# Expert stage: the split weights' tiles kept beside the load buffers, 14 load buffers in place of 15

## The chip, the cores and the metric

One core of a Trainium2 chip runs the whole program. The metric is the device time of one execution in microseconds (us), as the median of several runs. The engines are named as the profile names them: PE is TensorE's matmul, PEld its weight load, DVE is VectorE, ACT is ScalarE, POOL is GpSimd, SP is SyncE, which here issues the large loads.

## What is computed

The program is a two-block transformer over 256 tokens of width 1024. The first block has two layers (attention with a gated MLP, pooling, and a product-key expert layer each); the second block has a hybrid attention layer and, last of all, a mixture of 32 experts. Only that last stage changes its work, so it is the part of the reference that must be seen:

```python
def hier_moe(v, w_grp, b_grp, w_exp, b_exp, w_gate, w_up, w_down):
    ...
    w = p_grp * p_in / jnp.sum(p_in, axis=-1, keepdims=True)
    expert_id = g_sel * MOE_EXPERTS_PER_GROUP + e_sel
    combine = jnp.einsum('tk,tke->te', w, jax.nn.one_hot(expert_id, MOE_N_EXPERTS, dtype=f32))
    y = jnp.zeros(vt.shape, f32)
    for e in range(MOE_N_EXPERTS):
        hdn = jax.nn.silu(vt @ w_gate[e]) * (vt @ w_up[e])
        y = y + (combine[:, e:e + 1].astype(hdn.dtype) * hdn) @ w_down[e]
    return y.reshape(bsz, seq, d).astype(v.dtype)
```

Each token picks one of 4 groups and 2 of the group's 8 experts. A final root-mean-square norm follows.

## The kernel before, in words

**Weights before the expert stage.** Every large weight matrix comes in pieces of 128 partitions by 2048 columns (1024 KB). `raw` (L157) takes one of 3 load buffers of the pool `raw_p` and issues the load on SP's queue. `halves` (L164) cuts a piece in two and `split` (L148) writes each half as two rounded parts, a high one (ACT, L149) and a low one (DVE, L150), into tiles `hi` and `lo` of the pool `hl_p` (3 of each, 128 by 1024, 24 KB a partition in all). The last piece of work of this kind is `mix_out`, which multiplies by `w_out` (4 pieces) and computes the routing logits.

**Where the tiles lie.** `raw_p` is the second pool from the left end of the memory; `hl_p` stands at the right end (`side="right"`) in a stack of its own, `hl_es`, and is closed just before the expert stage. The stage's pool `rpool` then takes everything to the right of the room that is still in use: 10 load buffers `w0` to `w9`, and the rounded tiles `G`, `GT` and `yr`. `Carve` (L31) is a small allocator that cuts tiles out of large tiles that exist already; the other tiles of the stage are cut that way out of rooms of the layers before.

**The expert stage, `moe` (L1443).** The weights of 32 experts are 6 pieces each, 192 loads of 1024 KB, all on SP's queue, issued by `load` (L1458) in the order in which they are used. Load `j` goes into buffer `j` modulo the length of a ring `buf`: 3 of `raw_p`, 10 of `rpool`, 2 of the room, which are 15. A load waits on SP's queue until PE has done the last matmul on the buffer's old contents, and loads behind it wait with it.

The experts are done in 16 pairs, n = 0 to 15. Two experts of 64 token places each share the 128 columns of TensorE: `e = 0` works on the left half, `e = 1` on the right. One pair is, on PE:

- H, `hidden` (L1587): 32 matmuls for gate and up, 4 units of 2 loads each;
- S, `scatters` (L1621): 8 matmuls that add the pair before to the token sums;
- G, `places` and `gather` (L1551): 32 matmuls that gather the tokens of the next four experts, in every second pair (even n below 14);
- T, `hid_T` (L1598): 4 transposes, which need DVE's product of gate and up (L1592);
- B, `back` (L1569, L1571): 4 small matmuls for the pair after;
- D, `down` (L1611): 16 matmuls, 2 units of 2 loads; ACT (L1614) and DVE (L1615) write the two rounded halves of each result, which S reads.

Each matmul of H and D leaves two records in the trace, so that D is 32 records.

**What sets the order.** The program is written in the order H, S, G, T, B, D, but a scheduler orders the instructions of each engine when the kernel is built, by its own estimates of when operands are ready. It is free to put the S and G of a pair between the matmuls of D and H, and PE then runs its queue strictly in that order. The same scheduler orders SP's queue. After the 16 pairs a conditional block (L1668) handles experts with more than 64 tokens; here it is skipped. `final` (L1699) norms and writes the output.

Of the kernel before, what the change touches and what calls it, by code (L numbers as in the profile page):

```python
# [9 lines left out]
F32 = mybir.dt.float32  # L10
F32R = mybir.dt.float32r
# [6 lines left out]
P = 128  # L18
T = 256
# [11 lines left out]
class Carve:  # L31


    def __init__(self, *ranges):
        self.free, self.tags = [[t, lo * 256, hi * 256] for t, lo, hi in ranges], {}

    def tile(self, shape, dt=F32, name=None, tag=None, bufs=1):
        n = int(np.prod(shape[1:]))
        tag = tag or name
        if tag not in self.tags:  # L40
            w = -(-n // 8) * 8
            fits = [r for r in self.free if r[2] - r[1] >= w * bufs]
            assert fits, (name, n, [r[2] - r[1] for r in self.free])
            r = fits[0]
            self.tags[tag] = [r[0], r[1], w, bufs, 0]
            r[1] += w * bufs
        t = self.tags[tag]
        base, lo, w, bufs, j = t
        assert n <= w, (name, n, w)
        t[4] = (j + 1) % bufs  # L50
        v = base[:shape[0], lo + j * w:lo + j * w + n]
        if dt != F32:
            v = v.bitcast(dt)
        if len(shape) > 2:
            ax = "abcdefg"[:len(shape) - 1]
            v = v.rearrange(f"p ({' '.join(ax)}) -> p {' '.join(ax)}", **dict(zip(ax, shape[1:])))
        return v
# [45 lines left out]
class Net:  # L103
    def __init__(self, es, tc, A):
        self.tc, self.nc, self.A = tc, tc.nc, A
        nc = self.nc
        ep = es.enter_context
        self.cpool = ep(tc.tile_pool(name="cpool", bufs=1))
        self.raw_p = ep(tc.tile_pool(name="raw_p", bufs=3))
        self.hl_es = ExitStack()  # L110
        self.hl_p = self.hl_es.enter_context(tc.tile_pool(name="hl_p", bufs=3, side="right"))
        self.rings()
        self.ps = ep(tc.tile_pool(name="ps", bufs=4, space=bass.MemoryType.PSUM))
        self.small = ep(tc.tile_pool(name="small", bufs=2))
        self.hhl_p = ep(tc.tile_pool(name="hhl_p", bufs=1))
        self.hh, self.hl = (self.hhl_p.tile([P, KD, T], F32R, name=n) for n in ("hh", "hl"))
        self.uid = 0
        c = self.cpool
        self.ident = c.tile([P, P], F32, name="ident")
        self.ones = c.tile([P, P], F32, name="ones")  # L120
        self.vecs = c.tile([P, NV], F32, name="vecs")
        self.mod = [c.tile([P, 48], F32, name=f"mod{l}") for l in range(2)]
        self.mhalf = c.tile([P, 2], F32, name="mhalf")
        nc.scalar.dma_start(self.vecs, A["vecs"])
        nc.scalar.dma_start(self.ident, A["ident"])
        self.iota = c.tile([P, P], F32, name="iota")
        nc.scalar.dma_start(self.iota, A["iota"].partition_broadcast(P))
        nc.vector.memset(self.ones, 1.0)
        nc.vector.memset(self.mhalf, -0.5)

        self.scr = None
# [1311 lines left out]
    def moe(self, x, state, pool, rpool, nring):  # L1443

        nc, A, tc = self.nc, self.A, self.tc
        mm = nc.tensor.matmul
        tl = lambda shape, name, dt=F32, tag=None: pool.tile(shape, dt, name=name, tag=tag or name)
        CAP = 64
# [2 lines left out]
        xf, parts, pl, br, tri = state  # L1451


        buf = [None] * 3 + [rpool.tile([P, 2048], F32, name=f"w{j}") for j in range(nring)]
        buf += [pool.tile([P, 2048], F32, name=f"w{nring + j}") for j in range(2)]
        nring = len(buf)
# [99 lines left out]
        xg_tags = cycle(("vT", "xg"))  # L1556

        def tiles(ne):
            return (rpool.tile([P, 2, ne, CAP], F32R, tag="G", bufs=2, name=self.nm("G")),
                    pool.tile([P, KD, ne, CAP], F32, tag=next(xg_tags), name=self.nm("xg")))  # L1560

        def back(G, cb):

            GT = rpool.tile([P, T], F32R, tag="GT", bufs=2, name=self.nm("GT"))
            cw = pool.tile([P, 1], F32, tag="cw", bufs=2, name=self.nm("cw"))
            ps = self.mm()
            pair = lambda tt: G[:, tt].bitcast(F32).rearrange("p e s -> p (e s)")
            for tt in range(2):
                nc.tensor.transpose(ps[:, tt * P:(tt + 1) * P], pair(tt), self.ident)  # L1569
            for tt in range(2):  # L1570
                mm(ps[:, T:T + 2], pair(tt), cb[:, tt], start=(tt == 0), stop=(tt == 1))  # L1571
            nc.vector.tensor_copy(GT, ps[:, :T])
            for e in range(2):
                o = slice(e * CAP, (e + 1) * CAP)
                nc.vector.tensor_copy(cw[o], ps[o, T + e:T + e + 1])
            return GT, cw

# [25 lines left out]
        def down(hT, W, cw):  # L1603

            ys = []
            for n in range(2):
                ps = self.mm()
                Ws = [next(W) for _ in range(2)]
                for f in range(4):
                    for e in range(2):  # L1610
                        mm(ps[e * CAP:(e + 1) * CAP, :], hT[:, f, e, :], Ws[e][:, f * 512:(f + 1) * 512],  # L1611
                           start=(f == 0), stop=(f == 3))
                y = rpool.tile([P, 2, 512], F32R, tag="yr", bufs=3, name=self.nm("y"))
                nc.scalar.activation(y[:, 0, :], ps, AF.Copy, scale=cw)  # L1614
                nc.vector.scalar_tensor_tensor(y[:, 1, :], ps, cw, y[:, 0, :].bitcast(F32), ALU.mult, ALU.subtract)  # L1615
                ys.append(y)
            return ys

        def scatter(a, GT, y, tt, start, stop):
            for j in range(2):  # L1620
                mm(a, GT[:, tt * P:(tt + 1) * P], y[:, j, :], start=start and j == 0, stop=stop and j == 1)  # L1621

# [19 lines left out]

        def scatters(n, GT, ys):
            for m, y in enumerate(ys):
                for tt in range(2):
                    scatter(accs[tt][m], GT, y, tt, n == 0, n == 15)
                if n == 15:
                    add(accs, m)

        for n in range(16):  # L1650
# [4 lines left out]
            GT, cw = bk  # L1655
# [3 lines left out]
            if n < 15:  # L1659
                m = n + 1  # L1660
                p = slice(2 * (m % 2), 2 * (m % 2) + 2)
# [6 lines left out]
        with tc.If(over > CAP):  # L1668
            with tc.For_i(0, 32, 1) as ei:
# [4 lines left out]
                for b in (1, 3):  # L1674
# [10 lines left out]
                    G, xg = tiles(2)  # L1685
# [4 lines left out]
                    GT, cw = back(G, cb2)  # L1690
# [142 lines left out]
def build(tc, A, out):  # L1833
    nc = tc.nc
    with ExitStack() as es:
        net = Net(es, tc, A)
# [13 lines left out]
        with tc.tile_pool(name="mix0", bufs=1) as pool:  # L1850
            net.scr = pool
            x = pool.tile([P, 2, D], F32, name="x")
# [20 lines left out]
        pool = Carve((net.S2[0], 24, 64), whole[1])  # L1873
# [9 lines left out]
        x, gb = net.ahead  # L1883
# [10 lines left out]
        pool = Carve(*whole)  # L1894
# [6 lines left out]
        x, gb = net.ahead  # L1901
# [17 lines left out]
        for tt in range(2):  # L1919
            a, b = q[:, tt:tt + 1], q[:, 2 + tt:3 + tt]  # L1920
# [11 lines left out]
        pool = Carve((net.S2[0], 8, 64))  # L1932
        state = net.mix_out(x, pool)
        ws.close()
        upper.close()
        net.hl_es.close()
        with tc.tile_pool(name="moe", bufs=1, reuse_waits="tile") as rpool:
            net.moe(x, state, pool, rpool, 10)
            net.final(x, out, pool)


# [13 lines left out]
```

## Time and profile before

| | |
|---|---|
| median of 3 runs | 2654.69 us (2653.91 to 2655.37) |
| the profiled execution's own time | 2655.24 us |
| its span, first to last instruction | 2653.5 us |
| PE busy over the span | 2556.4 us (96%) |
| DVE, ACT busy | 1672.7 us (63%), 1267.6 us (48%) |
| bytes moved | 598.26 MB, mean 225 GB/s |
| expert stage, first matmul of H to last S | about 2160 to 2641 us of the span |

The span is shorter than the execution's own time by 1.7 us, which lie around it. A share of busy time is an average over stages with different limits, so the expert stage is read by itself: by the idle time of PE and what ended it, by SP's queue, and by PE's instructions in order of time.

### The profile page before, as it was taken

Reading aid. Unit: us, or ns where it says so; the run is one execution under the profiler, and the core shown is the slowest. Engines: PE = TensorE matmul, PEld = TensorE weight load, DVE = VectorE, ACT = ScalarE, POOL = GpSimd, SP = SyncE. Lnnn points to the kernel's source line nnn. Section 1 sums busy time; section 2 is a strip of 40 time slices with the busy share of each in tenths; the row PEclk is TensorE's granted clock in tenths of the full one; section 3 lists DMA queues with packets and bytes.
Section 4 is the critical chain, followed back from the end, with each engine's and each line's share of the span. In section 5 each row is a group of like instructions: output and inputs, shape, how many; then the busy total and the mean of one; then the engine's idle time right before and its main releaser. Section 6 shows DMA issues by size and latency. Waiting matters only on the chain. (4 is left out here: it accounts for less than half of the span.)

```text
span 2653.5 us, 39872 instructions
## 1 busy us (share of the span) xinstructions
PE 2556.4 (96%) x15570; PEld 2053.0 (77%) x15570; DVE 1672.7 (63%) x3465; ACT 1267.6 (48%) x2335; POOL 24.6 (1%) x28
## 2 busy tenths in 40 slices
PE   8989999999999998999999999999899989999997
PEld 4679999999888887999999988888777854333332
DVE  3665998889669985499888966666677631111111
ACT  4544445887545544444588754445466521001010
POOL 0000000000000000000000000000000000000000
PEclk9999999999999999999999999999999989999999
DMA  6544555333669972454533365555442589999994
GB/s 256 201 164 169 180 182 184 132 139 128 237 224 391 374 262 82 160 190 175 191 128 136 136 218 196 183 196 197 144 162 97 185 349 421 421 417 402 411 412 185
DMA packets 86798, 598.26 MB, mean 225 GB/s; under 512 B 10431, under 2 KB 12367, under 8 KB 15695
## 3 DMA queue, kind: packets, MB, share of 16 engines
q1 hardware_dynamic: 80608, 583.73, 58.5%
q10 hardware_dynamic: 5998, 11.94, 1.3%
q8 instruction: 124, 2.03, 0.3%
q14 instruction: 68, 0.55, 0.1%
HBM read 592.49 MB, written 3.15 MB: 224 GB/s over the span
## 5 line engine op out<-in xcount | busy, mean ns | idle before, releaser
L150 DVE TENSOR_TENSOR lo<-raw,hi 128x1024 fp32r<-128x1024 f32 x580 | 705.9, 1219 | 286.3 <-ACT hi L149 282.9
L149 ACT CAST hi<-raw 128x1024 fp32r<-128x1024 f32 x580 | 604.0, 1044 | 463.4 <-PE mm L737 289.4
L736 PE MATMUL mm<-hh,hi 128*128 128x256 f32 x2048 | 589.2, 288 | 0.0
L738 PE MATMUL mm<-hh,lo 128*128 128x256 f32 x2048 | 580.4, 283 | 0.0
L737 PE MATMUL mm<-hl,hi 128*128 128x256 f32 x2048 | 580.1, 283 | 0.0
L174 PE MATMUL acc<-hi,hh 128*128 128x512 f32 (+1 forms) x1312 | 511.3, 394 | 2.1 <-ACT hh L149 1.6
L176 PE MATMUL acc<-hi,hl 128*128 128x512 f32 (+1 forms) x1312 | 511.9, 390 | 0.0
L175 PE MATMUL acc<-lo,hh 128*128 128x512 f32 (+1 forms) x1312 | 511.2, 390 | 0.0
L737 PEld LDWEIGHTS mm<-hl,hi 128*128 128x128 f32 x2048 | 393.4, 192 | 0.0
L736 PEld LDWEIGHTS mm<-hh,hi 128*128 128x128 f32 x2048 | 393.1, 192 | 0.0
L738 PEld LDWEIGHTS mm<-hh,lo 128*128 128x128 f32 x2048 | 392.8, 192 | 0.0
L174 PEld LDWEIGHTS acc<-hi,hh 128*128 128x128 f32 x1312 | 247.4, 189 | 53.7 <-issue 2.2
L176 PEld LDWEIGHTS acc<-hi,hl 128*128 128x128 f32 x1312 | 247.2, 188 | 49.6
L175 PEld LDWEIGHTS acc<-lo,hh 128*128 128x128 f32 x1312 | 247.7, 189 | 48.7 <-DVE lo L150 0.6
L149 ACT CAST hh<-room 128x256 fp32r<-128x256 f32 x272 | 109.4, 407 | 311.2 <-PE acc L175 302.6
L1587 PE MATMUL mm<-w,room 128*64 128x512 f32 x688 | 181.9, 595 | 0.0
L1592 DVE TENSOR_TENSOR room<-room,mm 128x512 f32<-128x512 f32 x16 | 11.0, 688 | 267.2 <-PE mm L1587 267.2
L150 DVE TENSOR_TENSOR hl<-room,hh 128x256 fp32r<-128x256 f32 x272 | 112.0, 423 | 88.1 <-ACT hh L149 87.3
L1614 ACT ACTIVATE y<-mm,room 128x512 fp32r<-128x512 f32 x32 | 22.0, 687 | 248.8 <-PE mm L1611 248.8
L788 PE MATMUL mm<-room 128*128 128x128 f32 x1024 | 132.1, 275 | 0.1
L1587 PEld LDWEIGHTS mm<-w,room 128*64 128x64 f32 x688 | 56.1, 137 | 91.9 <-issue 89.4
L788 PEld LDWEIGHTS mm<-room 128*128 128x128 f32 x1024 | 123.9, 192 | 0.5 <-ACT room L782 0.5
(467 smaller groups left out, 3072.3 us busy)
## 6 DMA issues: line engine op xcount, KB each, us to landing
w<-in_moe SPq DMA_DIRECT2D x129, 1024.0 KB, 11.2
raw<-in_dn SPq DMA_DIRECT2D x128, 1024.0 KB, 4.9
raw<-in_up SPq DMA_DIRECT2D x103, 1024.0 KB, 4.9
raw<-in_moe SPq DMA_DIRECT2D x39, 1024.0 KB, 10.4
room<-in_up SPq DMA_DIRECT2D x25, 1024.0 KB, 6.3
raw<-in_modt SPq DMA_DIRECT2D x24, 1024.0 KB, 6.7
room<-in_moe SPq DMA_DIRECT2D x24, 1024.0 KB, 10.7
raw<-in_w2in SPq DMA_DIRECT2D x18, 1024.0 KB, 4.8
```

The source lines that it names most:

```text
L149: self.nc.scalar.copy(hi, src)
L150: self.last_lo = self.nc.vector.tensor_tensor(lo, src, hi.bitcast(F32), ALU.subtract).ins
L174: mm(ps, xh, wh, start=start, stop=False)
L175: mm(ps, xh, wl, start=False, stop=False)
L176: mm(ps, xl, wh, start=False, stop=stop)
L736: mm(o, wh, hh[:, k, :], start=(k == 0), stop=False)
L737: mm(o, wh, hl[:, k, :], start=False, stop=False)
L738: mm(o, wl, hh[:, k, :], start=False, stop=(k == KD - 1))
L788: mm(ps[:, j * P:(j + 1) * P], B[:, j, :], Am[:, j, :], start=True, stop=True)
L1587: mm(ps[e * CAP:(e + 1) * CAP, :], xs[:, k, e, :], Ws[e][:, (k % 4) * 512:(k % 4 + 1) * 512], start=(k == 0), stop=(k == KD - 1))
L1592: nc.vector.tensor_tensor(g, g, out[1], ALU.mult)
L1614: nc.scalar.activation(y[:, 0, :], ps, AF.Copy, scale=cw)
```

## The change

1. `hl_p` is opened on the left, right behind `raw_p`, for the whole program; `hl_es` and its closing are gone. All pools that are opened later lie 24 KB further right.
2. In the expert stage the 3 `hi` and 3 `lo` tiles of `hl_p` are taken once and stay. `y` takes the `hi` tiles in turn; `G` and `GT` are cut out of the `lo` tiles by `Carve`, 2 of each, as many as before.
3. `rpool` holds load buffers alone, 9 in place of 10, so the ring is 3 + 9 + 2 = 14, and the loads run 12 ahead in place of 13 as the program is written.
4. `Carve.tile` compares the type with that of the tile that it cuts from, since `lo` is not of type f32.

```diff
--- before.py
+++ after.py
@@ -49,7 +49,7 @@
         assert n <= w, (name, n, w)
         t[4] = (j + 1) % bufs
         v = base[:shape[0], lo + j * w:lo + j * w + n]
-        if dt != F32:
+        if dt != base.dtype:
             v = v.bitcast(dt)
         if len(shape) > 2:
             ax = "abcdefg"[:len(shape) - 1]
@@ -107,8 +107,7 @@
         ep = es.enter_context
         self.cpool = ep(tc.tile_pool(name="cpool", bufs=1))
         self.raw_p = ep(tc.tile_pool(name="raw_p", bufs=3))
-        self.hl_es = ExitStack()
-        self.hl_p = self.hl_es.enter_context(tc.tile_pool(name="hl_p", bufs=3, side="right"))
+        self.hl_p = ep(tc.tile_pool(name="hl_p", bufs=3))
         self.rings()
         self.ps = ep(tc.tile_pool(name="ps", bufs=4, space=bass.MemoryType.PSUM))
         self.small = ep(tc.tile_pool(name="small", bufs=2))
@@ -1451,6 +1450,11 @@
         xf, parts, pl, br, tri = state
 
 
+        his, los = ([self.hl_p.tile([P, 1024], F32R, tag=t, name=self.nm(t)) for _ in range(3)] for t in ("hi", "lo"))
+        rt = Carve(*[(t, 0, 4) for t in los])
+        ybuf = cycle(his)
+
+
         buf = [None] * 3 + [rpool.tile([P, 2048], F32, name=f"w{j}") for j in range(nring)]
         buf += [pool.tile([P, 2048], F32, name=f"w{nring + j}") for j in range(2)]
         nring = len(buf)
@@ -1556,12 +1560,12 @@
         xg_tags = cycle(("vT", "xg"))
 
         def tiles(ne):
-            return (rpool.tile([P, 2, ne, CAP], F32R, tag="G", bufs=2, name=self.nm("G")),
+            return (rt.tile([P, 2, ne, CAP], F32R, tag="G", bufs=2, name=self.nm("G")),
                     pool.tile([P, KD, ne, CAP], F32, tag=next(xg_tags), name=self.nm("xg")))
 
         def back(G, cb):
 
-            GT = rpool.tile([P, T], F32R, tag="GT", bufs=2, name=self.nm("GT"))
+            GT = rt.tile([P, T], F32R, tag="GT", bufs=2, name=self.nm("GT"))
             cw = pool.tile([P, 1], F32, tag="cw", bufs=2, name=self.nm("cw"))
             ps = self.mm()
             pair = lambda tt: G[:, tt].bitcast(F32).rearrange("p e s -> p (e s)")
@@ -1610,7 +1614,7 @@
                     for e in range(2):
                         mm(ps[e * CAP:(e + 1) * CAP, :], hT[:, f, e, :], Ws[e][:, f * 512:(f + 1) * 512],
                            start=(f == 0), stop=(f == 3))
-                y = rpool.tile([P, 2, 512], F32R, tag="yr", bufs=3, name=self.nm("y"))
+                y = next(ybuf).rearrange("p (a d) -> p a d", a=2)
                 nc.scalar.activation(y[:, 0, :], ps, AF.Copy, scale=cw)
                 nc.vector.scalar_tensor_tensor(y[:, 1, :], ps, cw, y[:, 0, :].bitcast(F32), ALU.mult, ALU.subtract)
                 ys.append(y)
@@ -1933,9 +1937,8 @@
         state = net.mix_out(x, pool)
         ws.close()
         upper.close()
-        net.hl_es.close()
         with tc.tile_pool(name="moe", bufs=1, reuse_waits="tile") as rpool:
-            net.moe(x, state, pool, rpool, 10)
+            net.moe(x, state, pool, rpool, 9)
             net.final(x, out, pool)
```

No instruction of computation is added or removed. Lines of the changed kernel are 4 higher in `moe` (L1587 is L1591 there).

**SP's queue where the stage's loads begin.** Behind the last piece of `w_out` stand, before (`raw` are the 3 shared load buffers, `w_20285` to `w_20294` the buffers w0 to w9):

```order
L1462 DMA raw_20408<-in_moe 128x2048
L1462 DMA raw_20410<-in_moe 128x2048
L1462 DMA raw_20412<-in_moe 128x2048
L1462 DMA w_20285<-in_moe 128x2048
L1462 DMA w_20286<-in_moe 128x2048
L1462 DMA w_20287<-in_moe 128x2048
```

and with the change (`w_20290` to `w_20298` are w0 to w8):

```order
L1466 DMA w_20290<-in_moe 128x2048
L1466 DMA w_20291<-in_moe 128x2048
L1466 DMA raw_20410<-in_moe 128x2048
L1466 DMA w_20292<-in_moe 128x2048
L1466 DMA raw_20412<-in_moe 128x2048
L1466 DMA raw_20414<-in_moe 128x2048
L1466 DMA w_20293<-in_moe 128x2048
```

Three loads into `rpool` now stand ahead of the last `raw` loads, whose buffers the last pieces of `w_out` still fill. After w8 SP now also reads the count that the conditional block tests (L1671); before, it did so after the last load.

**PE's queue in pair 2, from the middle of H to D.** Before, S (`acc`) and G (`G_20706`) lie inside H:

```order
L1587 MATMUL mm_20654<-w_20293,room_1438 64x512
L1621 MATMUL acc_20351<-y_20637,GT_20519 128x512 x2
...
L1621 MATMUL acc_20354<-y_20651,GT_20519 128x512 x2
L1587 MATMUL mm_20654<-w_20294,room_1438 64x512
...
L1587 MATMUL mm_20675<-room_1438 64x512
L1551 MATMUL mm_20709<-G_20706,hh 128x256 x2
...
L1587 MATMUL mm_20675<-room_1438 64x512 x7
L1551 MATMUL mm_20729<-G_20706,hh 128x256 x2
...
L1587 MATMUL mm_20675<-raw_20589,room_1438 64x512
L1598 MATMUL mm_20749<-ident,room_1438 128x128 x4
```

With the change H runs through, then S, then all of G, then T:

```order
L1591 MATMUL mm_20669<-w_20290,room_1438 64x512
L1625 MATMUL acc_20355<-hi_20286,lo_20288 128x512 x2
...
L1625 MATMUL acc_20358<-hi_20284,lo_20288 128x512 x2
L1555 MATMUL mm_20704<-lo_20287,hh 128x256 x2
...
L1555 MATMUL mm_20734<-lo_20287,hl 128x256 x2
L1602 MATMUL mm_20744<-ident,room_1438 128x128 x4
L1573 MATMUL mm_20750<-ident,lo_20287 128x128 x2
```

The stretch of a pair is counted here from the first matmul of the D before it to that of its own D. In counts of matmuls, the stretch of pair 2 was D16 H9 S8 H8 G20 H7 G4 H1 G8 H7 T4 and is D16 H32 S8 G32 T4.

**PE's queue in pair 3, around the end of D.** Before, S is cut in two, one half inside D and one behind the first matmul of H:

```order
L1611 MATMUL mm_20780<-w_20286,room_1438 64x512
L1621 MATMUL acc_20351<-y_20777,GT_20617 128x512
...
L1611 MATMUL mm_20780<-w_20287,room_1438 64x512
L1587 MATMUL mm_20795<-w_20288,room_1438 64x512
L1621 MATMUL acc_20352<-y_20792,GT_20617 128x512
...
L1587 MATMUL mm_20795<-w_20289,room_1438 64x512
```

With the change D runs through:

```order
L1615 MATMUL mm_20772<-w_20294,room_1438 64x512
L1591 MATMUL mm_20785<-w_20295,room_1438 64x512
L1625 MATMUL acc_20355<-hi_20285,lo_20288 128x512 x2
L1625 MATMUL acc_20357<-hi_20285,lo_20288 128x512 x2
L1625 MATMUL acc_20356<-hi_20286,lo_20288 128x512 x2
L1591 MATMUL mm_20785<-w_20296,room_1438 64x512
...
L1625 MATMUL acc_20358<-hi_20286,lo_20288 128x512 x2
L1591 MATMUL mm_20785<-w_20297,room_1438 64x512
```

The stretch of pair 3 was D9 S4 D7 H1 S4 H31 T4 and is D16 H1 S6 H7 S2 H24 T4. Pairs 0, 1 and 4 to 15 keep their order on PE, apart from the names of the buffers, and so do ACT, DVE and POOL throughout and every engine before the expert stage.

## Rows read from the trace of the kernel before

**Rows 1.** Busy time in stretches; engines in us, then granted clock, DMA share, GB/s:

```profile
core 0: us, PE busy (x) PEld busy (x) DVE busy (x) ACT busy (x) POOL busy (x), PEclk, DMA share, GB/s
2120.00:2130.00 10.00, 10.00 (x46) 8.29 (x45) 7.07 (x8) 4.50 (x7) 0.00 (x0) 1.00 0.54 197
2140.00:2150.00 10.00, 1.04 (x10) 0.93 (x9) 8.51 (x34) 2.31 (x4) 4.63 (x2) 0.56 0.99 407
2200.00:2600.00 400.00, 374.26 (x1686) 148.90 (x1685) 49.08 (x102) 39.68 (x63) 0.00 (x0) 1.00 1.00 414
```

**Rows 2.** Waits from 2200 to 2600 us: us in total, times, longest:

```profile
PEld acc L1621 <- ACT y L1614: 30.5, 24, 1.7
PEld mm L1587 <- DMA w<-in_moe: 0.9, 3, 0.3
PEld mm L1611 <- DMA w<-in_moe: 0.4, 1, 0.4
```

**Rows 3.** Waits of SP's queue from 2160 to 2600 us:

```profile
SPq L1462 <- PE mm L1587: 234.2, 111, 17.8
```

**Rows 4.** Busy time by stretch of pairs 1 to 4; columns as rows 1:

```profile
2179.32:2203.45 24.13, 23.86 (x114) 10.81 (x115) 4.20 (x10) 1.97 (x3) 0.00 (x0) 1.00 1.01 420
2203.45:2235.38 31.93, 30.72 (x147) 14.20 (x147) 3.44 (x8) 4.31 (x7) 0.00 (x0) 1.00 1.01 421
2235.38:2263.47 28.09, 26.08 (x114) 9.41 (x115) 4.19 (x10) 1.97 (x3) 0.00 (x0) 1.00 1.01 421
2263.47:2297.33 33.86, 31.76 (x147) 13.42 (x147) 3.43 (x8) 4.31 (x7) 0.00 (x0) 1.00 1.01 421
```

**Rows 5.** Timeline of PE, pairs 0 to 2 (start us, us, instruction, [idle before]):

```profile
2173.96 0.50 PE L1551 MATMUL mm<-G,hh 128*128 128x256 f32 x2
2177.89 0.60 PE L1598 MATMUL mm<-ident,room 128*128 128x128 f32 x4
2186.21 0.59 PE L1587 MATMUL mm<-w,room 128*64 128x512 f32 x1
2200.07 2.11 PE L1621 MATMUL acc<-y,GT 128*128 128x512 f32 x8
2202.02 0.60 PE L1598 MATMUL mm<-ident,room 128*128 128x128 f32 x4
2203.45 7.09 PE L1611 MATMUL mm<-w,room 128*64 128x512 f32 x32 [0.27 <-issue]
2210.34 4.45 PE L1587 MATMUL mm<-w,room 128*64 128x512 f32 x18
2222.93 3.65 PE L1587 MATMUL mm<-room 128*64 128x512 f32 x14
2226.51 0.51 PE L1551 MATMUL mm<-G,hh 128*128 128x256 f32 x2
```

**Rows 6.** Timeline of PE, pair 3:

```profile
2239.86 1.52 PE L1621 MATMUL acc<-y,GT 128*128 128x512 f32 x4
2241.31 3.22 PE L1611 MATMUL mm<-w,room 128*64 128x512 f32 x13
2247.19 10.52 PE L1587 MATMUL mm<-w,room 128*64 128x512 f32 x48
2261.98 0.66 PE L1598 MATMUL mm<-ident,room 128*128 128x128 f32 x4 [0.85 <-DVE room L1592]
```

**Rows 7.** Timeline of SP's queue (DMA issues), start of the stage's loads:

```profile
2118.39 11.21 SPq L1462 DMA_DIRECT2D raw<-in_moe  x3
2129.70 16.24 SPq L1462 DMA_DIRECT2D w<-in_moe  x10
2163.76 3.76 SPq L1462 DMA_DIRECT2D raw<-in_moe  x3
```

**Rows 8.** Three raw loads at 2194 to 2197 us: issue, then time to landing:

```profile
L1462 SPq DMA_DIRECT2D raw<-in_moe x3: 328/383/383, 2193.7 to 2197.1; - x3
DMA to landing us min/median/max: 14.1/14.6/16.2
```

## The prediction

> **What bounds the kernel now.** The change alters work in the expert stage alone, so I read that stage: first the busy time by stretches, then the waits of PE, then those of SP's queue, then PE's instructions one by one.
>
> The stretches show two engines that both look full [rows 1]: from 2200 to 2600 us PE is busy for 374 of 400 us, and the DMA engines for all of it, at 414 GB/s. The waits tell which of them sets the pace. In these 400 us PE's weight loads waited for a load of weights four times, 1.3 us in all [rows 2]. SP's queue, on the other hand, waited 234 us for PE to give buffers back [rows 3]. So the loads run ahead of PE, and the end moves with PE.
>
> What PE loses shows when stretches are compared. The stretch of pair 1 takes 24.13 us, that of pair 3, with the same number of matmuls, 28.09; that of pair 2, with 32 gathers, takes 31.93, and that of pair 4, with as many, 33.86 [rows 4]. The difference is the order. Pair 1 runs D, H and S through. In the others S and G cut D and H at odd places. A cut leaves an e = 0 matmul without its e = 1 partner on the other half of the columns, and T comes right behind H and waits 0.85 us for DVE's product [rows 6].
>
> **The change, part by part.**
>
> *PE's order in pair 2* (now D16 H32 S8 G32 T4). Every piece has stood in the trace in the same neighbourhood [rows 5]: D16 is 2210.34 - 2203.45 = 6.89 us; H32 up to S is 2200.07 - 2186.21 = 13.86; S8 is 2202.02 - 2200.07 = 1.95; G32 is 2177.89 - 2173.96 = 3.93; T to D is 2203.45 - 2202.02 = 1.43. The sum is 28.06 in place of 31.93 [rows 4]: **-3.87 us**. T waits for nothing here, since S and G now cover DVE's product. Were that cover not enough, 0.85 us would come back.
>
> *PE's order in pair 3* (now D16 H1 S6 H7 S2 H24 T4). One matmul with its partner takes 6.89 / 16 = 0.43 us each. D9 up to S took 2239.86 - 2235.38 = 4.48 [rows 4, 6]; D16 H1 has eight matmuls more: 4.48 + 8 x 0.43 = 7.92. S6 is six eighths of 1.95, 1.46. H7 up to the next piece is 2226.51 - 2222.93 = 3.58 [rows 5]. S2 is half of S4: (2241.31 - 2239.86) / 2 = 0.73. H31 with the wait of T took 2261.98 - 2247.19 = 14.79 [rows 6]; 31 cost as much as 32, so H24 is 14.79 - 8 x 0.43 = 11.35. T to D is 2263.47 - 2261.98 = 1.49. The sum is 26.53 in place of 28.09: **-1.56 us**. This order does not stand in the trace, so it has bounds: at best pair 1's 24.13 with T's wait of 0.85, or -3.1; at worst 28.09, or 0. I take the sum, since the cuts are two as before. S waits for ACT's result 30.5 / 24 = 1.3 us on average [rows 2]; in the new order H1 and four matmuls of S, some 1.8 us, stand between the end of D and the matmul that needs its last result, so that wait should go, and the sum holds none.
>
> *One buffer fewer.* A load now takes the buffer that was filled 14 loads ago in place of 15. At 421 GB/s [rows 4] a load of 1.049 MB takes 2.49 us, and as the DMA engines are never idle from here on, each load behind the first round lands one place, 2.49 us, later in relation to PE's unchanged work. PE would feel it only where a load has less than that to spare. The tightest place is the last unit of H in pair 2, because PE now gets there sooner: at 2210.34 + 3 x 8 x 0.43 = 2220.66. Its second load now takes the place in the queue of the third load in [rows 8], which landed at 2197.1 + 16.2 = 2213.3. So 7.4 us are left, and later the slack grows rather than shrinks: pairs 3 and 4 take PE 28.09 + 33.86 = 62 us, their 24 loads 24 x 2.49 = 59.8. **0 us**; this cover is spent if landings slip by more than 7.4 us.
>
> *SP's order.* Three loads move ahead of loads that wait for the last pieces of `w_out`. They fall into a time when the DMA engines are half idle (share 0.54 from 2120 to 2130 us [rows 1]). PE uses the first of them not before some 2160 us, and after the ring is full SP waits for PE's first release, at 2163.76 [rows 7], as before: nothing gained. On SP three `raw` loads now stand behind three `w` loads; the `w` loads wait for work of the layer's mixing that is over when `w_out`'s first pieces run, so nothing is held up. SP reads the count of tokens in the idle time before 2163.76. **0 us.**
>
> *Tiles in other places.* `y`, `G` and `GT` keep shapes, types and numbers of buffers, so no instruction gets a new wait for a buffer. That addresses move has no price in any row; H on `w` and on the room, tiles far apart, run at the same pitch [rows 5]. I take 0, and keep 1 us on either side.
>
> *Sum.* -3.87 - 1.56 = -5.4 us. Against the profiled execution's own 2655.24 us that is 2649.8; that execution stands 0.55 us over the median of the runs, 2654.69, so the forecast for the median is **2649.3 us**. The bounds of pair 3 and of the addresses make 2646.7 to 2651.8 of it.
>
> **The rivals.**
>
> *A. The loads become the bound: slower.* Place: the four units of H in pair 2. If the load of the last unit lands after PE is there, PE follows the loads from then on. The gain of pairs 2 and 3 is swallowed, and the end comes one load later: 2654.69 + 2.49 = **2657.2**. For it speaks the DMA share of 1.00, against it 7.4 us to spare and PE's waits of 1.3 us in 400. It decides from the point where landings slip by 7.4 us. The Trainium skill's page Trace Analysis (Identifying the Most-Contended Engine) judges TensorE by the share of its weight loads and the DMAs by the bandwidth they use, not by PE's busy share. By that rule the DMAs would be the more contended here, with weight loads at 148.90 of 400 us and loads at 414 GB/s, and rival A would be the result; the trace's waits do not agree. Chance 0.07.
>
> *B. Part of the gain stays away.* Pair 3's new cuts cost as much as the old ones, and in pair 2 T or G waits for a PSUM buffer that ACT's copies give back. Then -1 to -4, **2650.7 to 2653.7**. For it: pair 3's order is only pieced together, and ACT's copies of G come in one burst. Against: pair 0 has the same burst, in 3.93 us. Chance 0.18.
>
> *C. The order is worth nothing*, because another engine's chain sets the end of the stage: **2654.7**. Against it: the engine that ends last in the stage is PE's S, and DVE and ACT are busy for 49 and 40 of 400 us [rows 1]. Chance 0.05.
>
> *D. Pair 3 runs as smoothly as pair 1:* -3.87 - 3.1 = -7.0, **2647.7**. Chance 0.09.
>
> **How the numbers follow.** The forecast has the remaining 0.61, and 2649.3 +- 1.2 within it. A measurement of this kernel can tell about 0.2%, or 5.3 us, from no change, so the line for "faster" is 2649.4, almost on the forecast itself. Faster is a good half of 0.61 and all of D, 0.44. Slower by over 0.2% would need 2660.0, beyond A; I leave 0.05 for what moved addresses or a worse fit of the loads could do. The rest is 0.51. The range leaves out A and the outer edge of D: 2647.0 to 2654.0.
>
> **What would show it.** In the profile after, the stretch of pair 2 should be near 28.1 us and that of pair 3 near 26.5, those of pairs 1 and 4 unchanged at 24.1 and 33.9, PE's waits for loads still under 3 us, T's wait gone in pair 2 only, and the last load should land nearer to its use. SP's first `w` loads should start before the `raw` loads, some 15 us earlier, without H starting earlier. The prediction is wrong if PE waits for loads in pair 2 (A), if stretches 2 and 3 are shortened but the end does not follow (C), or if anything before 2100 us changes its length (addresses).

## The result, and the profile after

The change makes the kernel faster by about 32 us: 2622.73 us, the median of four runs (2621.97 to 2625.37), against 2654.66 before; the ratio is 0.988, interval 0.986 to 0.990. The profiled execution took 2622.57 us, its span is 2620.8. I had forecast 2649.3 us, with a range from 2647.0 to 2654.0. The expert stage did what was forecast; five sixths of the gain came from a place where I had put nothing.

First the stage that the prediction is about. Busy time of the changed kernel by stretch, pairs 1 to 4, then 400 us of the stage (columns as in [rows 1]):

```profile
2152.05:2176.18 24.13, 23.86 (x115) 10.81 (x115) 4.20 (x10) 1.97 (x3) 0.00 (x0) 1.00 1.01 421
2176.18:2204.07 27.89, 27.63 (x146) 14.62 (x147) 3.42 (x8) 4.32 (x7) 0.00 (x0) 1.00 1.01 420
2204.07:2230.64 26.57, 25.41 (x114) 9.79 (x115) 4.19 (x10) 1.97 (x3) 0.00 (x0) 1.00 1.01 421
2230.64:2264.46 33.82, 31.72 (x147) 13.38 (x147) 3.44 (x8) 4.32 (x7) 0.00 (x0) 1.00 1.01 421
2173.00:2573.00 400.00, 375.73 (x1711) 151.92 (x1711) 50.53 (x107) 40.40 (x64) 0.00 (x0) 1.00 1.01 420
```

Pair 2 went from 31.93 to 27.89 us, pair 3 from 28.09 to 26.57 [rows 4]; pairs 1 and 4 stayed. That is 5.56 us. PE's timeline of the changed kernel shows the new order: in pair 2, S runs through, G follows it in one piece, and T waits for nothing; in pair 3, T still waits for DVE's product.

```profile
2196.93 2.11 PE L1625 MATMUL acc<-hi,lo 128*128 128x512 f32 x8
2198.88 0.40 PE L1555 MATMUL mm<-lo,hh 128*128 128x256 f32 x2
...
2202.65 0.60 PE L1602 MATMUL mm<-ident,room 128*128 128x128 f32 x4
2204.07 7.09 PE L1615 MATMUL mm<-w,room 128*64 128x512 f32 x32 [0.27 <-issue]
2210.96 1.02 PE L1591 MATMUL mm<-w,room 128*64 128x512 f32 x2
2211.91 1.66 PE L1625 MATMUL acc<-hi,lo 128*128 128x512 f32 x6
2213.51 3.65 PE L1591 MATMUL mm<-w,room 128*64 128x512 f32 x14
2217.09 0.73 PE L1625 MATMUL acc<-hi,lo 128*128 128x512 f32 x2
...
2229.16 0.66 PE L1602 MATMUL mm<-ident,room 128*128 128x128 f32 x4 [0.89 <-DVE room L1596]
```

The waits from 2173 to 2573 us (us in total, times, longest), PE's and then those of SP's queue from 2133 to 2573, say that PE still leads: it waited 4.1 us for loads, SP 321 us for PE.

```profile
PEld acc L1625 <- ACT hi L1618: 29.7, 24, 1.7
PEld mm L1591 <- DMA w<-in_moe: 2.0, 6, 0.4
PEld mm L1615 <- DMA w<-in_moe: 1.1, 3, 0.4
PEld mm L1591 <- DMA raw<-in_moe: 0.6, 2, 0.3
PEld mm L1615 <- DMA room<-in_moe: 0.4, 1, 0.4
...
SPq L1466 <- PE mm L1591: 192.4, 97, 9.6
SPq L1466 <- PE mm L1615: 128.6, 39, 7.9
SPq L1466 <- DMA w<-in_moe: 33.0, 22, 2.1
```

Before, from 2160 to 2600 us, SP waited 374 us for PE, by the line of [rows 3] and a second one, and 1.0 us for loads:

```profile
SPq L1462 <- PE mm L1611: 139.6, 40, 8.1
```

So SP has less to spare than before, 321 us in place of 374, and now waits 45 us in all for loads to land, but PE's own waits for loads stay at 1% of the stretch.

The rest is found by cutting both spans at like instructions of PE. The cuts are the first matmul of a peer layer's queries, the first of its second half (up), the same again for layer 1, and the start of pair 1. First the kernel before, then the changed one (columns as in [rows 1]):

```profile
190.74:671.27 480.53, 480.49 (x4040) 480.27 (x4039) 395.93 (x981) 302.20 (x622) 0.00 (x0) 1.00 0.45 157
671.27:1055.35 384.08, 373.81 (x1666) 308.94 (x1665) 293.08 (x451) 185.73 (x281) 3.65 (x4) 0.99 0.71 269
1055.35:1535.52 480.17, 480.15 (x4041) 479.90 (x4039) 396.10 (x981) 302.17 (x622) 0.00 (x0) 1.00 0.45 156
1535.52:2179.32 643.80, 620.20 (x3076) 502.20 (x3075) 415.23 (x690) 339.68 (x565) 12.30 (x11) 0.98 0.53 190
2263.47:2653.50 390.03, 351.80 (x1562) 135.81 (x1562) 52.23 (x106) 39.33 (x63) 1.38 (x2) 0.99 0.91 374
```

```profile
190.84:654.78 463.94, 463.40 (x4040) 462.64 (x4039) 394.64 (x981) 302.38 (x622) 0.00 (x0) 1.00 0.46 162
654.78:1041.76 386.98, 376.80 (x1667) 308.59 (x1665) 293.21 (x451) 185.70 (x281) 3.65 (x4) 0.99 0.71 267
1041.76:1505.25 463.49, 463.05 (x4040) 462.10 (x4039) 394.79 (x981) 302.50 (x622) 0.00 (x0) 1.00 0.46 162
1505.25:2152.05 646.80, 623.43 (x3076) 501.33 (x3075) 415.14 (x690) 339.81 (x565) 12.89 (x11) 0.98 0.52 187
2230.64:2620.80 390.16, 351.64 (x1562) 135.58 (x1562) 52.25 (x106) 39.37 (x63) 1.38 (x2) 0.99 0.92 383
```

The queries and the first half (dn) of each peer layer became 16.6 and 16.7 us shorter, the two long stretches behind them 2.9 and 3.0 us longer. With 0.1 us ahead of the layers, pairs 2 and 3, and 0.1 behind, that is the whole: 0.1 - 16.6 + 2.9 - 16.7 + 3.0 - 5.6 + 0.1 = -32.8; the spans differ by 32.7. In the peer layers each engine's instructions and their waits are the same in the same order, the clock granted is 1.00 in both, and PE is busy all the time in both (but for 0.5 us in the changed one), with as many matmuls. So PE's matmuls themselves became quicker. The groups of PE's three costliest lines, before and then after (busy us, mean ns):

```profile
L736 PE MATMUL mm<-hh,hi 128*128 128x256 f32 x2048 | 589.2, 288 | 0.0
L738 PE MATMUL mm<-hh,lo 128*128 128x256 f32 x2048 | 580.4, 283 | 0.0
L737 PE MATMUL mm<-hl,hi 128*128 128x256 f32 x2048 | 580.1, 283 | 0.0
```

```profile
L735 PE MATMUL mm<-hh,hi 128*128 128x256 f32 x2048 | 577.0, 282 | 0.0
L737 PE MATMUL mm<-hh,lo 128*128 128x256 f32 x2048 | 568.0, 277 | 0.7 <-DVE lo L149 0.7
L736 PE MATMUL mm<-hl,hi 128*128 128x256 f32 x2048 | 567.4, 277 | 0.0
```

Each is 6 ns shorter. A matmul's end is modelled and the matmuls overlap, so for the pace I count matmuls in a window: from 330 to 430 us, within the first half of layer 0, PE has 836 before and 870 after, one in 119.6 ns and one in 114.9. (A count takes in the two or three that began ahead of the window, so it reads some 0.3 ns too quick.) In the trace two of these matmuls in a row start 120 ns apart in nearly every case before. After, there are two paces, 113.3 and 117.8 ns, and each holds for a while. Two windows of 20 us within the 100 show them (columns: us, PE busy (x), PEclk, DMA share, GB/s); the kernel before has 169 in both:

```profile
360.00:380.00 20.00, 20.00 (x179) 1.00 0.54 197
410.00:430.00 20.00, 20.00 (x172) 1.00 0.54 189
```

Between them, at 405 us, PE waits 0.34 us for a tile `lo` and goes on at the slower pace. A layer has 384 of these matmuls in the queries and 3072 in the first half: 3456 x 4.7 ns = 16.2 us, close to the 16.6 that were missing. Those of 512 columns, which stream hi or lo on weights of hh or hl, started 227 ns apart before, and 226 to 232, on average 229, after: over the 1536 of a layer's second half that is what the long stretches lost.

What the change moved: hi and lo lie at the right end of the memory before (hi at byte 204,768 of a partition, hh at 44,000), and between the load buffers and hh after (43,808 and 68,576). Did the place matter, or the distance?

### The profile page after: what moved, and what is told of

The parts are those of the page before. It is cut to its first block, busy times and chain, and to the rows that moved or that the text cites. A ratio compares the mean times of both kernels' runs of the same rounds, so it can differ in the third digit from the quotient of the medians.

```text
span 2620.8 us, 39871 instructions
## 1 busy us (share of the span) xinstructions
PE 2524.7 (96%) x15570; PEld 2016.3 (77%) x15570; DVE 1670.3 (64%) x3465; ACT 1268.2 (48%) x2335; POOL 25.2 (1%) x28
## 5 line engine op out<-in xcount | busy, mean ns | idle before, releaser
L735 PE MATMUL mm<-hh,hi 128*128 128x256 f32 x2048 | 577.0, 282 | 0.0
L737 PE MATMUL mm<-hh,lo 128*128 128x256 f32 x2048 | 568.0, 277 | 0.7 <-DVE lo L149 0.7
L736 PE MATMUL mm<-hl,hi 128*128 128x256 f32 x2048 | 567.4, 277 | 0.0
L737 PEld LDWEIGHTS mm<-hh,lo 128*128 128x128 f32 x2048 | 385.3, 188 | 1.4 <-DVE lo L149 1.1
L736 PEld LDWEIGHTS mm<-hl,hi 128*128 128x128 f32 x2048 | 385.4, 188 | 0.0
L735 PEld LDWEIGHTS mm<-hh,hi 128*128 128x128 f32 x2048 | 384.9, 188 | 0.0
L1591 PE MATMUL mm<-w,room 128*64 128x512 f32 x640 | 169.9, 595 | 0.0
L1618 ACT ACTIVATE hi<-mm,room 128x512 fp32r<-128x512 f32 x32 | 22.0, 687 | 241.6 <-PE mm L1615 241.6
L1591 PEld LDWEIGHTS mm<-w,room 128*64 128x64 f32 x640 | 52.5, 137 | 91.4 <-issue 88.2
```

Of the source, the lines that this page charges most:

```text
L735: mm(o, wh, hh[:, k, :], start=(k == 0), stop=False)
L736: mm(o, wh, hl[:, k, :], start=False, stop=False)
L737: mm(o, wl, hh[:, k, :], start=False, stop=(k == KD - 1))
L1591: mm(ps[e * CAP:(e + 1) * CAP, :], xs[:, k, e, :], Ws[e][:, (k % 4) * 512:(k % 4 + 1) * 512], start=(k == 0), stop=(k == KD - 1))
```

## The experiments

Theory A: the pace depends on the distance between the tile that streams and the tile that is loaded as weights, modulo some power of two. Before the change hh minus hi was a multiple of 1,024; after it is 24,768, or 192 more than one. Theory B: it depends on the part of the memory, or on the neighbours. The instruments are small tiles (the pool `small` and tiles of the constants' pool) that can lie on either side of the big ones: hh and hi move by at most 1,152 bytes against each other. In all but e13 and e14 the instructions, their order and their waits stay, and in e1 to e14 hi, lo, hh and hl begin at multiples of 32 bytes. "D" is the distance from hi to hh modulo 256; lo lies 12,288 bytes behind hi and hl 8,192 behind hh, so lo and hl have the same D, except in e12.

**e1_small_first**, D = 0, hi and lo between the load buffers and hh as in the change, but 192 bytes further right:

```diff
+        self.small = ep(tc.tile_pool(name="small", bufs=2))
         self.raw_p = ep(tc.tile_pool(name="raw_p", bufs=3))
         self.hl_p = ep(tc.tile_pool(name="hl_p", bufs=3))
...
-        self.small = ep(tc.tile_pool(name="small", bufs=2))
```

> The changed kernel with the 192 bytes of the small tiles put ahead of the load buffers: hi and lo stay between the load buffers and hh, but the distance from hi to hh is 24,576 bytes (a multiple of 1,024, as it was before the change) in place of 24,768. Theory A (the pace of TensorE hangs on the distance between the tile that streams and the tile that is loaded as weights, modulo 1,024 or a divisor of it): the peer layers' matmuls of 256 columns go back from 113.5 to 120 ns, and the kernel to about 2649 us, the time before less the 6 us of the expert stage. Theory B (it hangs on which part of the memory hi and lo lie in, or beside which tiles): 113.5 ns stays, and 2622.7 us within 2 us.

**e2_before_hh192**, the kernel before with hh and hl 192 bytes lower:

```diff
+        self.hhl_p = ep(tc.tile_pool(name="hhl_p", bufs=1))
+        self.hh, self.hl = (self.hhl_p.tile([P, KD, T], F32R, name=n) for n in ("hh", "hl"))
         self.small = ep(tc.tile_pool(name="small", bufs=2))
-        self.hhl_p = ep(tc.tile_pool(name="hhl_p", bufs=1))
-        self.hh, self.hl = (self.hhl_p.tile([P, KD, T], F32R, name=n) for n in ("hh", "hl"))
```

> The kernel before with hh and hl moved down by 192 bytes and nothing else: hi and lo stay at the right end, 160,960 bytes from hh in place of 160,768 (which was a multiple of 1,024). Theory A: the peer layers' matmuls of 256 columns go from 120 to about 113.5 ns, and the kernel to about 2628 us. Theory B: 120 ns and 2654.7 us within 2 us.

**e3_d32** and **e4_d64**, like e1 with the 32 bytes of `mhalf`, or the 64 of `silu_c`, between lo and hh:

```diff
         self.hl_p = ep(tc.tile_pool(name="hl_p", bufs=3))
+        self.cp2 = ep(tc.tile_pool(name="cp2", bufs=1))
...
-        self.mhalf = c.tile([P, 2], F32, name="mhalf")
+        self.mhalf = self.cp2.tile([P, 2], F32, name="mhalf")
```

> The changed kernel with hh 24,608 bytes behind hi (32 bytes over a multiple of 1,024). Theory A: if 32 bytes are enough to part the two tiles, about 113.5 ns and 2622 us; if the tiles meet in a wider unit, 120 ns and 2649 us. Theory B: 2622.7 us within 2 us, whatever the distance.

> The changed kernel with hh 24,640 bytes behind hi (64 bytes over a multiple of 1,024). Theory A: as with 192 bytes, about 113.5 ns and 2622 us, if the unit in which the tiles meet is 128 bytes or less, since 192 is 64 modulo 128; 120 ns and 2649 us if it is wider. Theory B: 2622.7 us within 2 us.

Measured: e1 2649.48 us (ratio to the kernel before 0.9977, interval 0.9968 to 0.9987), e2 2661.82 (1.0025, 1.0016 to 1.0035), e3 2649.37 (0.9978, 0.9969 to 0.9988), e4 2656.30 (1.0005, 0.9995 to 1.0014). Stretches of e1: queries and first half of layer 0, then pairs 2 and 3, then the counting windows of PE alone (its columns: us, PE busy (x), PEclk, DMA share, GB/s):

```profile
190.66:670.93 480.27, 480.24 (x4041) 480.01 (x4039) 395.90 (x981) 302.21 (x622) 0.00 (x0) 1.00 0.44 157
2202.87:2230.83 27.96, 27.69 (x147) 14.70 (x147) 3.44 (x8) 4.32 (x7) 0.00 (x0) 1.00 1.01 420
2230.83:2257.39 26.56, 25.41 (x115) 9.81 (x115) 4.19 (x10) 1.97 (x3) 0.00 (x0) 1.00 1.01 421
330.00:430.00 100.00, 100.00 (x836) 1.00 0.52 181
1600.00:1700.00 100.00, 100.00 (x443) 1.00 0.55 191
```

With 192 bytes moved, the layer is back at 480.27 us and 836 matmuls in 100 us, and the short pairs 2 and 3 stay. So B falls, as hi and lo still lie between the load buffers and hh, and e1 is the forecast by itself: the order of the expert stage without the moved distance. But e2 is no 2628: at 2661.82 us it is slower than either theory had said, with paces of its own. e3 and e4 missed the numbers that A had named as well: e3 comes to the time of e1 by other paces (860 and 430 in the table below). The counting windows of e2, then of e4:

```profile
330.00:430.00 100.00, 100.00 (x852) 1.00 0.54 190
1600.00:1700.00 100.00, 100.00 (x431) 1.00 0.53 188
```

```profile
330.00:430.00 100.00, 100.00 (x851) 1.00 0.52 189
1600.00:1700.00 100.00, 100.00 (x430) 1.00 0.53 188
```

They are alike: 118 ns for the 256 columns and 233 for the 512 in both, with hi at the right end in one and beside the load buffers in the other. In e2 the distance is 192 less than a multiple of 1,024, in e4 it is 64 more. The two are the same modulo 256 (or 128), though each tile by itself lies elsewhere: hi 224 and hh 32 bytes over a multiple of 256 in e2, 160 and 224 in e4. Their times differ by 5.5 us, about what the expert stage is worth, which only e4 has. What the pace repeats with was the next question.

**e5_d128**, **e6_d256**, **e7_d512**, **e8_d96**: other tiles moved behind lo in the same way; in e6 `small` stays behind lo and `silu_c` joins it, in the others `small` lies ahead as in e1:

```diff
-        self.vecs = c.tile([P, NV], F32, name="vecs")
-        self.mod = [c.tile([P, 48], F32, name=f"mod{l}") for l in range(2)]
+        self.vecs = self.cp2.tile([P, NV], F32, name="vecs")
+        self.mod = [self.cp2.tile([P, 48], F32, name=f"mod{l}") for l in range(2)]
...
-        self.sc = self.cpool.tile([P, 16], F32, name="silu_c")
+        self.sc = self.cp2.tile([P, 16], F32, name="silu_c")
```

This is e5; e6 moves `silu_c` alone, e7 `iota`, e8 `silu_c` and `mhalf`.

> The changed kernel with hh 25,728 bytes behind hi (128 bytes over a multiple of 1,024). What the pace repeats with is in question. Theory A128 (what counts is the distance modulo 128): the paces of distance 0, 120 ns for the 256 columns and 227 ns for the 512, and about 2649 us. Theory A1024 (modulo 1,024, or 256 or 512): paces of their own, between those of 64 bytes (118 and 233) and of 192 bytes (113.5 and 229), and 2620 to 2656 us.

> The same with 256 bytes over a multiple of 1,024. Theory A128, or one with 256: 120 and 227 ns, 2649 us. Theory A1024, or one with 512: other paces, 256 columns at 118 ns or less.

> The same with 512 bytes over a multiple of 1,024. Theory A128, or one with 256 or 512: 120 and 227 ns, 2649 us. Theory A1024: other paces, 256 columns at 118 ns or less.

> The same with 96 bytes over a multiple of 1,024. Theory A128: the paces lie near those of 32 bytes (117 and 234 ns) if the distance counts alike in both directions; Theory A1024: between the paces of 64 and of 192 bytes, 256 columns at 114 to 118 ns. 2620 to 2656 us.

Measured, one execution each beside 2653.18 us of the kernel before: 2666.93, 2653.22, 2648.97 and 2675.61 us. At 256 and at 512 bytes the paces are those of distance 0 again (120 and 227 ns); at 128 they are not (118 to 122, and 232). So a period of 128 falls by e5, of 512 or 1,024 by e6, and 256 is left, which had also put e2 and e4 together. e5's time lies above what the wider periods had named. For e8 both theories had named paces of their own, and both missed that of the 256 columns (835 and 428 in the table below); it is the slowest version of all.

**e9_d160**, **e10_d224**, the two steps of 32 bytes that were left (e9: the two `mod` tiles and `mhalf` moved, `small` ahead; e10: `mhalf` moved, `small` behind lo); **e11_before_hh64**, the kernel before with D = 192; **e12_lo_apart**, D = 0 for hi and 192 for lo:

```diff
 # e11
         self.hh, self.hl = (self.hhl_p.tile([P, KD, T], F32R, name=n) for n in ("hh", "hl"))
+        self.cp2 = ep(tc.tile_pool(name="cp2", bufs=1))
...
-        self.sc = self.cpool.tile([P, 16], F32, name="silu_c")
+        self.sc = self.cp2.tile([P, 16], F32, name="silu_c")
 # e12, and the same at line 1453
         self.hl_p = ep(tc.tile_pool(name="hl_p", bufs=3))
+        self.cp2 = ep(tc.tile_pool(name="cp2", bufs=1))
+        self.lo_p = ep(tc.tile_pool(name="lo_p", bufs=3))
...
-            hi, lo = (self.hl_p.tile([P, 1024], F32R, tag=t, name=self.nm(t)) for t in ("hi", "lo"))
+            hi, lo = (p.tile([P, 1024], F32R, tag=t, name=self.nm(t)) for p, t in ((self.hl_p, "hi"), (self.lo_p, "lo")))
...
-        self.sc = self.cpool.tile([P, 16], F32, name="silu_c")
+        self.sc = self.cp2.tile([P, 16], F32, name="silu_c")
```

> The changed kernel with hh 24,992 bytes behind hi, 160 over a multiple of 256. Theory A256 (the pace repeats with 256 bytes): a pace of its own, which no row so far gives; between the neighbours of 128 (120 and 232 ns) and 192 bytes (113.5 and 229 ns), 2623 to 2667 us. A theory by which only the distance to the nearest multiple of 256 counts would put it with 96 bytes: about 123 and 234 ns, 2675 us.

> The same with 224 over a multiple of 256. Theory A256: between the neighbours of 192 (113.5 and 229 ns) and 0 bytes (120 and 227 ns), 2623 to 2649 us. The nearest-multiple theory would put it with 32 bytes: 117 and 234 ns, 2649 us.

> The kernel before with the 64 bytes of one small tile moved from ahead of hh to behind hl, so that hh lies 192 over a multiple of 256 from hi, as the change had it, hi and lo stay at the right end, and the expert stage and its ten buffers are as before. Theory A256: the peer layers' matmuls at 113.5 ns, and 2655 less 26.8 (the difference of the distance-0 version of the change and the change) = 2628 us. Theory B (the part of the memory): 120 ns and 2655 us.

> The changed kernel with 64 bytes put between hi and lo: hi lies 0 and lo 192 over a multiple of 256 from hh and hl. Of the three matmuls of each group of the peer layers, the first (L735 of the changed kernel) streams hh on hi and is followed by one that loads hi, the second streams hl on hi and is followed by one that loads lo, the third streams hh on lo and is followed by one that loads hi. Theory 'next' (a matmul that streams is slowed by the load of the next weights): the second at 113.5 ns, the first and third at 120. Theory 'own' (by its own weights): the third at 113.5 ns, the others at 120. Theory 'not TensorE alone' (by the engines that write hi and lo): no such split among the three.

Measured: e9 2660.56 us (ratio 1.002, 1.0011 to 1.003) and e10 2660.46 (1.0017, 1.0007 to 1.0027); e10 lies outside its neighbours' bounds, so between the steps nothing can be interpolated. The nearest-multiple theory falls with both: 845 and 847 matmuls, where e8 and e3 have 835 and 860. e11 2635.84 us (0.9929, 0.9913 to 0.9946): moving one tile of 64 bytes in the kernel before wins some 19 us, the converse of e1, though 8 us less than expected. Its stretches for the queries and first halves of the two layers, 14.7 and 14.9 us shorter than before and 1.9 and 1.8 longer than in the change:

```profile
191.55:657.37 465.82, 465.39 (x4041) 464.62 (x4039) 394.64 (x981) 302.29 (x622) 0.00 (x0) 1.00 0.46 162
1043.27:1508.53 465.26, 464.82 (x4040) 463.88 (x4039) 394.84 (x981) 302.40 (x622) 0.00 (x0) 1.00 0.47 161
```

This execution spans 2630.6 us, and its four runs lie between 2632.47 and 2639.10, wider than the change's. Part of the reason stands in the trace: from 460 to 560 us, where the change keeps to its quicker pace and has 885 matmuls, e11 goes to and fro between 113 and 118 ns every few us, and has 874:

```profile
460.00:560.00 100.00, 100.00 (x874) 1.00 0.40 140
```

What makes it change there stays open. e12 (2653.45 us, one execution): all three matmuls start 117 to 119 ns apart. That is near the mean of two at 119.6 and one at 113.5 (117.6), which "next" and "own" both give, but spread evenly over the three. No split is what "not TensorE alone" had named; the next two runs are the test of that.

**e13_alone_d0** and **e14_alone_d192**: e1 and the change without the loads and splits that feed the peer layers:

```diff
-            for u in range(NI // 2):
-                yield from self.halves(A[w][l, u])
+            one = next(self.halves(A[w][l, 0]))
+            for u in range(NI):
+                yield one
```

> The version at distance 0 (e1_small_first) without the work that feeds the peer layers' matmuls: each of the two weight arrays is loaded and split for its first half unit alone, and all 128 steps use that one pair of tiles. Theory 'TensorE alone' (its stream is slowed by its own loading of weights): 120 ns for the 256 columns and 227 for the 512 stay, though no split and no load of weights runs beside them. Theory 'feeders' (the engines or transfers that write hi, lo and the load buffers slow it): both come clearly below, towards 107 and 213 ns, a column per cycle at the clock of 2.4 GHz.

> The changed kernel (distance 192) with the same work left out. Theory 'TensorE alone': 113 to 114 ns and 226 to 231 stay, so that the two runs differ by about 6.5 ns in each matmul of 256 columns, as the complete kernels do. Theory 'feeders': the same paces as e13_alone_d0.

One execution each: 2646.25 and 2618.20 us, 28 us apart as the complete kernels (2649.48 and 2622.73, 27 us). Counting windows of e13, then of e14:

```profile
330.00:430.00 100.00, 100.00 (x836) 1.00 0.00 1
```

```profile
330.00:430.00 100.00, 100.00 (x885) 1.00 0.01 1
```

With the DMA engines and DVE idle and ACT busy for a tenth of the window, the pace at distance 0 is the same 119.6 ns, and at 192 it is 113.0. In e13, some 2600 of these matmuls ran with neither ACT nor DVE busy, 120 ns apart. So the loads and the splits are needed for neither pace: theory "feeders" falls, and TensorE with the two tiles that it reads is left. That the change has 870 in this window and e14 885 does not show that the feeders cost something at 192. Without them e14 has the two paces too, 113.5 ns in the first of these windows and 117.8 in the second (some matmuls of another form lie between in both):

```profile
500.00:600.00 100.00, 100.00 (x886) 1.00 0.01 1
1320.00:1420.00 100.00, 100.00 (x865) 1.00 0.01 1
```

Over the whole of both layers, such matmuls that follow each other without a wait start 114.3 ns apart on average in the change and 114.4 in e14. The Trainium skill's page SBUF — State Buffer (A bandwidth-pool intuition that's wrong) gives LDWEIGHTS a read port of its own, independent of the one that streams; by that rule the distance should be worth nothing. The 836 and 885 here do not agree, and the measurement decides.

**e15_d208** and **e16_d200**: 16 and 8 bytes on top of the change's 192, with `mhalf` laid into the rest of `vecs` to make room:

```diff
-        self.hh, self.hl = (self.hhl_p.tile([P, KD, T], F32R, name=n) for n in ("hh", "hl"))
+        both = self.hhl_p.tile([P, 2 * KD * T + 8], F32R, name="hh")[:, 4:4 + 2 * KD * T]
+        self.hh, self.hl = (both[:, j * KD * T:(j + 1) * KD * T].rearrange("p (k t) -> p k t", t=T) for j in range(2))
```

(In e16 the offset is 2 in place of 4.)

> The changed kernel with hh and hl 16 bytes further, 208 over a multiple of 256 from hi and lo. If the pace is set in units of 32 bytes: as with 192, 113.5 and 229 ns, 2622 us within 3. If finer: between 192 and 224 (117 and 234 ns, 2660 us), about 2640 us, or below 2622.

> The same with 8 bytes, 200 over a multiple of 256. Units of 32 or of 16 bytes: as with 192, 2622 us within 3. If finer: between, 2622 to 2640 us, or below.

Measured: 2661.81 us (1.0026, 1.0016 to 1.0036) and 2662.25 (1.0029, 1.0019 to 1.0040). Eight bytes undo the gain, more than any expectation allowed. But these are the only two versions in which hh and hl do not begin at a multiple of 32 bytes. Whether the distance or that start costs the gain is not shown: no run moves hi and lo by 8 bytes along with them. In one table, by distance modulo 256 (matmuls from 330 to 430 us, of 256 columns; from 1600 to 1700, of 512 but for the row of 192):

| D | kernels | 330 to 430 | 1600 to 1700 | us |
|---|---|---|---|---|
| 0 | e1, e6, e7 | 836, 836, 835 | 443 | 2649.5, 2653.2, 2649.0 |
| 0 | before | 836 | 443 | 2654.7 |
| 32 | e3 | 860 | 430 | 2649.4 |
| 64 | e4, e2 | 851, 852 | 430, 431 | 2656.3, 2661.8 |
| 96 | e8 | 835 | 428 | 2675.6 |
| 128 | e5 | 836 | 432 | 2666.9 |
| 160 | e9 | 845 | 431 | 2660.6 |
| 192 | the change, e11 | 870, 870 | 443, 444 | 2622.7, 2635.8 |
| 200, 208 | e16, e15 | 836, 841 | 435, 433 | 2662.3, 2661.8 |
| 224 | e10 | 847 | 430 | 2660.5 |

Before, e2 and e11 keep the expert stage of before, the others that of the change. At 192 the second count has 16 shorter matmuls in it, here those of the change,

```profile
L271 PE MATMUL mm<-room,ones 128*128 128x128 f32 x16 | 2.9, 296 | 0.0
```

and its matmuls of 512 columns start 229 ns apart, where 443 at distance 0 stands for 227. No complete version beats the change: by luck, it hit the one good distance of ten.

## Why the prediction was wrong

- **Pair 2, -3.87 us: right.** It came to 28.06 by the sum and 27.89 in the trace; T's wait is gone, as the step said.
- **Pair 3, -1.56 us: right.** 26.53 by the sum, 26.57 measured. T waits 0.89 us there, and rival D (7.0 us from both pairs) did not come.
- **One buffer fewer, 0 us: right.** PE waited 4.1 us for loads in 400, where I had said under 3; that sign missed. Before it was 1.6: the 1.3 of [rows 2] leaves out 0.3 for a `raw` load. SP's wait for PE is 321 us against 374; the 234 of [rows 3] is one of two lines. Rival A did not come.
- **SP's order, 0 us: right.** Its first `w` loads start at 2086.94 us and no longer at 2129.70 [rows 7], 43 us earlier, of which 27 are the shift of all that lies ahead, so some 15 by themselves, as I had said. Next to nothing was gained by it: from the start of the mixing's last matmul to pair 1 it took 44.7 us before, 44.1 in the change and 44.6 in e1, which has the same order.

```profile
2086.94 0.81 SPq L1466 DMA_DIRECT2D w<-in_moe  x2
2091.54 0.33 SPq L1466 DMA_DIRECT2D raw<-in_moe  x1
```

- **Tiles in other places, "I take 0, and keep 1 us on either side": wrong.** This is the step that failed. It was worth -27.3 us by the stretches, 27 by e1 against the change, and as such outside every rival; the one chance left to moved addresses, 0.05, was for a slower kernel. The reason given, that H on `w` and on the room ran at one pitch, compared matmuls of another form, with weights of 64 columns, and the step asked only for tiles whose instructions the change touches. The change also moved `hi` and `lo` against `hh` and `hl`, the operands of the kernel's most frequent matmuls, in stretches where PE is busy for 480.5 of 480.5 us. A pace that hangs on such a distance could not be read in one trace with one layout, but a bound could: the matmuls of 512 columns started 227 ns apart, so 256 columns should need half of that, 113.5 by this estimate, and they took 119.6. Some 6 ns in each of 6912 matmuls, 42 us, had no cause that the profile named, and that was no ground for +-1. The Trainium skill's page TensorE: Matmul & The Clock Gate (Back-to-back issue gap) gives 256 / 2.4 + 2.5 = 109 ns for such a matmul by itself; by it the estimate of what had no cause would have been 10.4 ns each, 72 us. The best pace that a run here holds is 113.3 ns.
- **The sign that was named held:** "if anything before 2100 us changes its length (addresses)". All of the surplus lies there.

Without that term the forecast is e1: 2649.48 us, where 2649.3 was predicted.

## What to carry to other kernels

When a change moves tiles, look at the distance between the operand that streams and the one that is loaded as weights in the matmuls that fill the time, not only at the tiles of the edited stage; modulo 256 bytes it was worth 53 us of 2650 here (2622.7 to 2675.6, the latter one execution). Where PE is busy without a wait and its matmuls still start further apart than their columns take, shift one of the two tiles by steps of 32 bytes with a small tile between them, and count matmuls of one form in several windows for each, since one distance can have two paces. Keep a version that does only the move apart from the one that does the rest: e1 and e11 split this gain in two runs.

## What was not expected of the hardware

- The pace of matmuls with 256 columns and 128 columns of weights, both fp32r, hung on the distance of the two tiles modulo 256 bytes: in 100 us, 870 (114.9 ns) to 835 (119.8) in the complete kernels, and 885 against 836 without the feeders. With 512 columns it was 227 ns at distance 0 to 234 at 96, and the order of the distances is another: 0 is the best for 512 columns and among the worst for 256.
- It is not the distance alone. At 0 the matmuls of 256 columns started 120 ns apart and at 64 118 ns apart throughout, but at 192 there were two paces, 113.3 and 117.8 ns, in one and the same execution (179 and 172 in 20 us). The change of pace at 405 us came with a wait of PE; whether the wait made it is not shown. Only the quicker pace sets 192 apart: the slower is that of 64.
- It does not change smoothly: 192 gave 870 matmuls in 100 us and 224 gave 847; 200 gave 836 and 208 gave 841, with tiles that do not begin at a multiple of 32 bytes.
- The place in the memory had little to do with it: e2 and e4 agree within 1 in 850, the change and e11 give 870 both, though in one of each hi lies some 160,000 bytes from hh, in the other some 24,700. That the two reads meet in the same piece of the memory is an explanation that fits, but no run shows it, nor whether a matmul is slowed by its own weights or by the load of the next.
